# Q and k by 256-column matmuls in two PSUM banks, and the first column pairs of both retention output projections by seven products

## The chip, the cores and the metric

One core of one Trainium2 chip runs the kernel. The metric is the device time of one execution in microseconds (us). Three runs of the kernel before took 1381.68, 1379.70 and 1380.17 us; their median is 1380.17 us. The profile comes from one further execution.

## What is computed

A trunk of two layers over 256 tokens (`SEQ`) of width 2048 (`D`), all in float32: a gated linear attention layer (GLA, 4 heads) and a retention layer (8 heads). Each normalises its input, projects it to q, k, v and a gate, mixes the tokens head by head, multiplies by the gate's SiLU and projects back, with a residual add:

```python
def retention_mixer(h, positions, w_in, gn_g, gn_b, w_out):
    proj = h @ w_in
    q, k, v, gate = jnp.split(proj, [RET_DK, 2 * RET_DK, 2 * RET_DK + D_INNER], axis=-1)
    ...
    return (o * jax.nn.silu(gate)) @ w_out

def reference(x, ...):
    h = x
    for i in range(DEPTH):
        ...
            h = h + gla_mixer(rms_norm(h, gla_norm[j]), ...)
        ...
            h = h + retention_mixer(rms_norm(h, ret_norm[j]), ...)
    return rms_norm(h, final_norm)
```

With 256 tokens nearly all the work is in the projections: the input projections (2048 x 10240 for GLA, 2048 x 12288 for retention) and the two output projections (4096 x 2048).

## The kernel before

**Splitting.** Every float32 factor is split into a high part and a low part (`hi`, `lo`), and each product is the sum of three matmuls, high by high, high by low and low by high. `xhl` holds both parts of the layer's input for all 16 blocks of 128 rows (`kt`), `ogt` those of the gated output of the current half of the heads. Weights come as blocks of 256 rows by 512 columns (512 KB). SP loads a block into one of eight buffers (`emit_raw`, L228), ScalarE copies it to `hi` (L283), VectorE subtracts to get `lo` (L284). The order of all blocks is planned ahead by `_plan` (L56): `loads` is the order of the loads, `subs` the order of use. Splits run three blocks ahead of the matmuls (`LOOK`), loads at least six (`DMA_LOOK`).

**Plain column groups.** `steps_x` (L330) takes a block, and for each of two token halves `t` and two row blocks `q` issues three matmuls of 512 columns (`mm3`, L321 to L323): 12 matmuls of 512 columns per block, 8 blocks per group of 512 output columns.

**Pairs by seven products.** Two column groups that need the same input (v and gate of one head, or two neighbouring output columns) can be computed together on their first 1024 rows by Strassen's scheme: the upper four row blocks of both, for both token halves, make a two by two product of blocks, done in seven products instead of eight. `product` (L397) takes two combined weight blocks and issues 12 matmuls; `direct` (L404) takes the four remaining blocks of each group plainly. Tokens in order `P1 v4 z P3 ...` say which comes when: P1 to P8 are the products, v4 to v7 and g4 to g7 the plain blocks of the two groups. Weights are combined by DMAs on GpSimd's queue that add a second block into a loaded one (L292, `post`) and by VectorE adds (L278); the input is combined by `make_sums` (L420), which builds four token sums with their splits, called f3, f5, f6, f7. A pair takes 84 + 96 = 180 matmuls where two plain groups take 192, and 22 splits where they take 16. `JOINT` (L152) says which column groups go in pairs: `("ro", half)` is the retention output projection of a half of the heads, with one entry for columns 0 and 1 and one for columns 2 and 3.

**Q and k.** `step_w` (L342) computes q and k of a head transposed: the weights stand in the array, and the 256 tokens stream through. For each of four output blocks `c` and two row blocks it issues one matmul with the high weights over 512 columns (high and low part of x side by side, L364) and one with the low weights over 256 columns (L365). Each `c` has a PSUM bank of its own, with two halves of 256 columns; `evac_w` (L377) and `qk_done` (L1250) add the two halves: a ScalarE copy (L1257) and a VectorE add (L1258) for each `c`. There are 12 heads, 8 blocks each: 768 such pairs of matmuls.

**Order around the change.** GLA heads 0 and 1 (`gla_head`), the first half of the GLA output projection (`out_half`, tiles `gae`), GLA heads 2 and 3, its second half, then retention heads 0 to 3, the output projection `ra` of that half, heads 4 to 7, `rb`, and `out_tail`. Within a retention head the order is `WHOLE` for heads 0 and 4 (all q and k first) and `MIXED` for the others. The rest of a head (`ret_tasks`: scores, norm, transposes into `ogt`) is cut into steps that `step` runs between matmul blocks of the head itself and of what comes next. In `ra` and `rb`, columns 0 and 1 run plainly, first six blocks of each and then the last two (`CUT`), so that the last head's output has time to arrive; the residual is read back (`get_resid`) between these. In `ra`, columns 2 and 3 are a pair, its token sums (`rsum`) being made in steps during head 3 and `ra`'s first columns; `rb` has no pair. PSUM has eight banks: four named by `slots` (`acc`), two in the pool `lev`, two in `mis`.

## Time and profile before

| | |
|---|---|
| median of three runs | 1380.17 us |
| the profiled execution: its own time | 1379.47 us |
| its span, first to last instruction | 1377.6 us |
| busy: TensorE matmuls | 1366.5 us in 6632 records |
| busy: VectorE, ScalarE | 1079.1 us, 836.0 us |
| granted TensorE clock, mean | 0.998 |

In the profile PE is TensorE's matmuls, PEld its weight loads (they overlap the matmuls), DVE is VectorE, ACT ScalarE, POOL GpSimd, SP the engine that issues most loads. A line of the timeline gives start and duration in us. A matmul's duration holds its passage through the array, which overlaps the next matmul's: how fast matmuls follow each other is read from their starts, not from their durations. In a table by windows, the number behind x counts what touches the window, and the last three columns are the granted clock, the share of the 16 DMA engines that was busy, and what they moved.

### The profile page before, as it was taken

How to read it: one execution, taken by the hardware profiler on the slowest of the kernel's cores; microseconds unless marked ns; L12 is line 12 of the kernel's file. 1: busy time of each engine (PE TensorE's matmuls, PEld its weight loads, DVE VectorE, ACT ScalarE, POOL GpSimd, SP SyncE). 2: the span in 40 equal slices, each digit the busy share in tenths (PEclk: the TensorE clock that was granted, in tenths of full speed). 3: DMA queues.
4: the chain of work that ended last, by engine and by line, in shares of the span. 5: the costliest groups of instructions: out<-in, count | busy, mean ns of one | idle time of the engine just before them, and what ended most of it. 6: DMA issues, size and time to landing. Idle time of an engine off the chain costs nothing.

```text
span 1377.6 us, 18438 instructions
## 1 busy us (share of the span) xinstructions
PE 1366.5 (99%) x6632; PEld 1148.5 (83%) x6632; DVE 1079.1 (78%) x1497; ACT 836.0 (61%) x1104; POOL 131.8 (10%) x188
## 2 busy tenths in 40 slices
PE   9999999999999999999999999999999999999997
PEld 7888888888888888888888888888888888888887
DVE  6686795987878896769888888886858897888673
ACT  6576656656567747656666566655546666666452
POOL 1003020110021021001011010100101101010000
PEclk9999999999999999999999999999999999999999
DMA  9765556689658657858897878896798797879661
GB/s 359 245 182 160 172 177 187 151 250 343 204 153 265 204 175 180 314 168 247 279 317 202 256 203 247 208 310 206 184 372 238 217 271 193 256 199 327 211 191 62
DMA packets 83931, 312.94 MB, mean 227 GB/s; under 512 B 9712, under 2 KB 10736, under 8 KB 82560
## 3 DMA queue, kind: packets, MB, share of 16 engines
q1 hardware_dynamic: 67344, 242.64, 50.9%
q0 software_dynamic: 15056, 61.74, 22.6%
q10 hardware_dynamic: 1440, 7.38, 1.4%
q8 instruction: 52, 0.85, 0.2%
q14 instruction: 39, 0.32, 0.1%
HBM read 301.24 MB, written 10.49 MB: 226 GB/s over the span
## 4 chain that ended last, share of the span: by engine, by line
PE 99%; DMA 0%; DVE 0%; ACT 0%; DVEq 0%; issue 0%; SPq 0%
PE rqk_ps L364 8%; PE re_ps L392 8%; PE re_ps L391 8%; PE re_ps L393 8%; PE rqk_ps L365 4%; PE gqk_ps L364 4%; PE gg_ps L322 3%; PE gv_ps L321 3%; PE gv_ps L322 3%; PE gv_ps L323 3%; PE gg_ps L323 3%; PE gg_ps L321 3%; PE ge_ps L392 2%; PE ge_ps L393 2%; PE ge_ps L391 2%; PE gae_ps L391 2%
## 5 line engine op out<-in xcount | busy, mean ns | idle before, releaser
L284 DVE TENSOR_TENSOR lo<-raw,hi 128x1024 fp32r<-128x1024 f32 (+1 forms) x557 | 675.2, 1222 | 225.7 <-ACT hi L283 218.9
L283 ACT ACTIVATE hi<-raw 128x1024 fp32r<-128x1024 f32 (+1 forms) x557 | 584.5, 1056 | 390.8 <-PE gg_ps L323 49.0
L364 PE MATMUL rqk_ps<-xhl,hi 128*128 128x512 f32 x480 | 162.8, 397 | 0.0
L392 PE MATMUL re_ps<-lo,xhl 128*128 128x512 f32 x352 | 137.3, 390 | 0.0
L393 PE MATMUL re_ps<-hi,xhl 128*128 128x512 f32 x352 | 137.1, 390 | 0.0
L391 PE MATMUL re_ps<-hi,xhl 128*128 128x512 f32 x352 | 132.7, 391 | 0.0
L292 POOL DMA_DIRECT2D raw<-in_w_all x84 | 72.7, 867 | 530.3 <-DVE lo L284 283.8
L365 PE MATMUL rqk_ps<-xhl,lo 128*128 128x256 f32 x480 | 122.3, 280 | 0.0
L364 PEld LDWEIGHTS rqk_ps<-xhl,hi 128*128 128x128 f32 x480 | 89.5, 188 | 17.9
L365 PEld LDWEIGHTS rqk_ps<-xhl,lo 128*128 128x128 f32 x480 | 87.5, 189 | 3.4
L393 PEld LDWEIGHTS re_ps<-hi,xhl 128*128 128x128 f32 x352 | 66.1, 188 | 13.6
L391 PEld LDWEIGHTS re_ps<-hi,xhl 128*128 128x128 f32 x352 | 66.1, 188 | 13.3
L392 PEld LDWEIGHTS re_ps<-lo,xhl 128*128 128x128 f32 x352 | 66.1, 188 | 13.1
L364 PE MATMUL gqk_ps<-xhl,hi 128*128 128x512 f32 x216 | 76.5, 398 | 0.0
L322 PE MATMUL gg_ps<-lo,xhl 128*128 128x512 f32 x192 | 75.4, 393 | 0.0
L322 PE MATMUL gv_ps<-lo,xhl 128*128 128x512 f32 x192 | 75.2, 392 | 0.0
L321 PE MATMUL gv_ps<-hi,xhl 128*128 128x512 f32 x192 | 75.1, 393 | 0.0
L323 PE MATMUL gv_ps<-hi,xhl 128*128 128x512 f32 x192 | 75.0, 391 | 0.0
L323 PE MATMUL gg_ps<-hi,xhl 128*128 128x512 f32 x192 | 74.9, 390 | 0.0
L321 PE MATMUL gg_ps<-hi,xhl 128*128 128x512 f32 x192 | 74.8, 391 | 0.0
L365 PE MATMUL gqk_ps<-xhl,lo 128*128 128x256 f32 x216 | 59.0, 280 | 0.0
L801 POOL TENSOR_TENSOR s<-s,m 128x64 f32<-128x64 f32 x56 | 36.1, 676 | 232.7 <-DVE m L792 223.4
(407 smaller groups left out, 2682.5 us busy)
## 6 DMA issues: line engine op xcount, KB each, us to landing
raw<-in_w_all SPq DMA_DIRECT2D x451, 512.0 KB, 4.8
raw<-in_w_all POOLq DMA_DIRECT2D x84, 512.0 KB, 6.5
resid<-in_x_n SPq DMA_DIRECT2D x2, 1024.0 KB, 9.1
gg<-in_gn_g POOLq DMA_DIRECT2D x8, 256.0 KB, 3.9
resid_x<-resid ACTq DMA_DIRECT2D x1, 2048.0 KB, 9.1
gb<-in_gn_b POOLq DMA_DIRECT2D x8, 256.0 KB, 6.2
gb_resid<-resid_x POOLq DMA_DIRECT2D x1, 2048.0 KB, 11.8
resid_g<-gb_resid ACTq DMA_DIRECT2D x1, 2048.0 KB, 8.9
```

The lines of the kernel that those rows point to most:

```text
L283: a = nc.scalar.activation(hi[:, sl], src[:, sl], AF.Copy)
L284: b = nc.vector.tensor_tensor(lo[:, sl], src[:, sl], hi[:, sl].bitcast(F32), ALU.subtract)
L292: nc.gpsimd.dma_start(raws[n], block(key), accum_op=ALU.add)
L321: mm(ps, xh, hi[:, q, :], start=kt == 0, stop=False)
L322: mm(ps, xh, lo[:, q, :], start=False, stop=False)
L323: mm(ps, xl, hi[:, q, :], start=False, stop=kt == NKT - 1)
L364: mm(ps[c], wh, rhs[:, kt, :, :], start=kt == 0, stop=False)
L365: mm(ps[c][:, 0, :], wl, rhs[:, kt, 0, :], start=False, stop=False)
L391: mm(ps, xh, hi[:, q, :], start=start, stop=False, **again)
L392: mm(ps, xh, lo[:, q, :], start=False, stop=False, **again)
L393: mm(ps, xl, hi[:, q, :], start=False, stop=stop, **again)
L801: nc.gpsimd.tensor_tensor(dst, dst, side_of(m[:, li, :], z), ALU.add)
```

## The change

Three things are changed.

1. **Q and k.** Each pair of matmuls (512 and 256 columns) becomes three of 256: high weights by the high part of x, high weights by the low part, low weights by the high part, all three into the same 256 columns of PSUM. Two blocks `c` share a bank, so that q and k of a head take two banks instead of four. The two halves need not be added afterwards: two ScalarE copies of 512 columns replace four copies and four VectorE adds.
2. **Pairs.** `("ro", 0)` becomes (True, True) and `("ro", 1)` (True, False): columns 0 and 1 of `ra` and of `rb` are pairs (tiles `rae`, `rbe`). They run in the order `LATE`, in which the plain blocks of the last head (v6, v7, g6, g7) come late and the second gate accumulator has a bank of its own in `lev`. `CUT` is gone.
3. **Token sums.** They are made in head 2 of each half (heads 2 and 6) instead of around `ra`; two of the four go to DRAM at once (`spill_sums`) and come back at the end of heads 3 and 7 (`back_sums`). `get_resid` moves to v7 of those heads. In the order `MIXED`, P2 comes before q4, and P5 gets bank C.

How the order of instructions changes at three places (names with numbers are single tiles; `hi` and `lo` are the split weight blocks).

TensorE, in the q and k of retention head 0 (`rqk_ps` are its accumulators, one for each output block before, one for two blocks after): before, a high matmul of 512 columns and a low one of 256 alternate,

```order
L364 MATMUL rqk_ps_5767<-xhl,hi_5801 128x512
L365 MATMUL rqk_ps_5767<-xhl,lo_5802 128x256
L364 MATMUL rqk_ps_5764<-xhl,hi_5801 128x512
L365 MATMUL rqk_ps_5764<-xhl,lo_5802 128x256
L364 MATMUL rqk_ps_5765<-xhl,hi_5801 128x512
L365 MATMUL rqk_ps_5765<-xhl,lo_5802 128x256
```

and now:

```order
L365 MATMUL rqk_ps_5984<-xhl,hi_5942 128x256
L366 MATMUL rqk_ps_5984<-xhl,hi_5942 128x256
L368 MATMUL rqk_ps_5984<-xhl,lo_5943 128x256
L365 MATMUL rqk_ps_5984<-xhl,hi_5942 128x256
L366 MATMUL rqk_ps_5984<-xhl,hi_5942 128x256
L368 MATMUL rqk_ps_5984<-xhl,lo_5943 128x256
```

The columns are the same, 768 for each block; there are three instructions for them instead of two, and the first two carry the same weights.

TensorE, where the first half of the GLA output projection begins (`gg_ps` is the last gate of head 1, `got_tp` are transposes of a head's output, `gae_ps` the first product P1; the brackets name what an instruction waits for): before,

```order
L323 MATMUL gg_ps_2118<-hi_2230,xhl 128x512
L679 MATMUL got_tp_2267<-ident,go_1984 128x128 [waits DVE_49]
L679 MATMUL got_tp_2295<-ident,go_1984 128x128
L391 MATMUL gae_ps_2326<-hi_2250,ogt 128x512 [waits Activation_49]
L679 MATMUL got_tp_2267<-ident,go_1984 128x128 [waits DVE_49]
L679 MATMUL got_tp_2267<-ident,go_1984 128x128 x2
L679 MATMUL got_tp_2295<-ident,go_1984 128x128 x3
```

and now:

```order
L333 MATMUL gg_ps_2228<-hi_2340,xhl 128x512
L709 MATMUL got_tp_2377<-ident,go_2094 128x128 [waits DVE_49]
L709 MATMUL got_tp_2405<-ident,go_2094 128x128
L709 MATMUL got_tp_2377<-ident,go_2094 128x128 [waits DVE_49]
L709 MATMUL got_tp_2377<-ident,go_2094 128x128 x2
L709 MATMUL got_tp_2405<-ident,go_2094 128x128 x3
L400 MATMUL gae_ps_2436<-hi_2360,ogt 128x512 [waits Activation_49]
```

Since GLA head 0 now takes two banks of `slots` where it took four, the groups after it lie in the other two banks: P1's bank is now that of the gate just finished, and P1 stands behind all eight transposes.

GpSimd's queue of DMAs, from the end of head 3 through `ra` (`raw` rows are weight blocks that are added into loaded ones; `resid` is the residual, `dm`, `gg`, `gb` are constants of the next head): before,

```order
L460 DMA ra_resid<-resid_g 128x4096
L1162 DMA dm_9376<-in_dmat 128x384
L1169 DMA gb_9403<-in_gn_b 128x512
L1168 DMA gg_9823<-in_gn_g 128x512
L292 DMA raw_8374<-in_w_all 128x1024
L292 DMA raw_8394<-in_w_all 128x1024
```

and now:

```order
L490 DMA resid_8540<-resid_g 128x4096
L1206 DMA dm_9900<-in_dmat 128x384
L447 DMA rsum_8682<-rsum_kept 128x2048
L1213 DMA gb_9927<-in_gn_b 128x512
L300 DMA raw_8495<-in_w_all 128x1024
L300 DMA raw_8507<-in_w_all 128x1024
L1212 DMA gg_10401<-in_gn_g 128x512
L300 DMA raw_8581<-in_w_all 128x1024
L300 DMA raw_8593<-in_w_all 128x1024
L300 DMA raw_8495<-in_w_all 128x1024
L300 DMA raw_8507<-in_w_all 128x1024
```

The six adding DMAs of the first pair (`raw_8495` to `raw_8593`) and the return of the two spilled sums (`rsum_8682`) are new; those of the second pair (`raw_8374` before) follow behind them.

The diff, cut to its core:

```diff
--- before.py
+++ after.py
@@ _plan
-                        post.append((x[j], (g, 2 + j)))
+                        (owed if " ".join(order) == LATE else post).append((x[j], (g, 2 + j)))
...
-    def out_cols_of(name, half, cut, joint):
+    def out_cols_of(name, half, joint):
...
-MIXED = "q0 q1 P1 q2 q3 q4 z P5 q5 P6 q6 q7 P2 P3 v4 v5 v6 P7 v7 g4 g5 P8 g6 g7"
+MIXED = "q0 q1 P1 q2 q3 P2 q4 z P5 q5 P6 q6 q7 P3 v4 v5 v6 P7 v7 g4 g5 P8 g6 g7"
...
+LATE = "v4 g4 P1 v5 z P3 g5 P5 v6 P6 P2 g6 P7 v7 g7 P8"
...
-CUT = 6
 EARLY = 2
 JOINT = {
     "a": (5, 7),
     ("ao", 0): (True, True),
     ("ao", 1): (False, True),
-    ("ro", 0): (False, True),
-    ("ro", 1): (False, False),
+    ("ro", 0): (True, True),
+    ("ro", 1): (True, False),
 }
@@ step_w
+        at = lambda c: ps[c // 2][:, c % 2, :]
+        both = lambda c: {"skip_group_check": c % 2 == 1}
...
-            if kt == NKT - 1:
-                mm(ps[c][:, 0, :], wl, rhs[:, kt, 0, :], start=False, stop=False)
-                mm(ps[c], wh, rhs[:, kt, :, :], start=False, stop=True)
-            else:
-                mm(ps[c], wh, rhs[:, kt, :, :], start=kt == 0, stop=False)
-                mm(ps[c][:, 0, :], wl, rhs[:, kt, 0, :], start=False, stop=False)
+            a = [
+                lambda c=c, wh=wh, kt=kt: mm(at(c), wh, rhs[:, kt, 0, :], start=kt == 0 and c % 2 == 0, stop=False, **both(c)),
+                lambda c=c, wh=wh, kt=kt: mm(at(c), wh, rhs[:, kt, 1, :], start=False, stop=False, **both(c)),
+            ]
+            b = [lambda c=c, wl=wl, kt=kt: mm(at(c), wl, rhs[:, kt, 0, :], start=False, stop=kt == NKT - 1, **both(c))]
...
-        ps = ps or acc(4, f"{name}_ps", (P, 2, SEQ))
+        ps = acc(2, f"{name}_ps", (P, 2, SEQ))
...
-    def evac_w(ps, dst, name):
-        tmp = t4_p.tile([P, 4, SEQ], F32, tag="t4", name=f"{name}_h2")
+    def evac_w(ps, dst):
         with tc.high_priority():
-            for c in range(4):
-                nc.scalar.activation(tmp[:, c, :], ps[c][:, 1, :], AF.Copy)
-                halves = lambda a: a.rearrange("p (z t) -> p z t", z=2)
-                to = dst[:, c // 2, :].rearrange("p (z k t) -> p z k t", z=2, k=2)[:, :, c % 2, :]
-                nc.vector.tensor_tensor(to, halves(ps[c][:, 0, :]), halves(tmp[:, c, :]), ALU.add)
+            for i in range(2):
+                to = dst[:, i, :].rearrange("p (z k t) -> p k z t", z=2, k=2)
+                nc.scalar.activation(to, ps[i].rearrange("p k (z t) -> p k z t", z=2), AF.Copy)
@@ make_sums
+    def sums_apart(name):
+        def room(n):
+            if n == 0:
+                return v_p.tile([P, 2, QK, 2, P], F32R, tag="v", name=f"{name}0")
+            return [t4_p.tile([P, QK, 2, P], F32R, tag="t4", name=f"{name}_t{i}") for i in range(2)]
+
+        return room
+
+    def spill_sums(name):
+        kept = dram_p.tile([P, 2 * QK * 2 * P], F32R, tag=name, name=f"{name}_kept")
+        for i in range(2):
+            nc.gpsimd.dma_start(
+                kept[:, i * QK * 2 * P : (i + 1) * QK * 2 * P], cur["next_s"][2 + i].rearrange("p k a t -> p (k a t)")
+            )
+        cur["spilt"] = kept
+
+    def back_sums(name):
+        two_ = v_p.tile([P, 2, QK, 2, P], F32R, tag="v", name=f"{name}1")
+        nc.gpsimd.dma_start(two_.rearrange("p i k a t -> p (i k a t)"), cur["spilt"])
+        cur["next_s"][2:4] = [two_[:, 0], two_[:, 1]]
+
+    def make_sums(lhs, name, where, key="s"):
+        s = cur[key] = [None] * 4
         room = where(name)
@@ out_pair
+        order = out_order(name[0] + "o", c)
+        G1 = A
+        if order == LATE:
+            G1 = lev_p.tile([P, GW], F32, tag="lev", name=f"{name}e{c}_g1")
...
+        toks = [x for x in order.split() if x != "z"]
+        for n, tok in enumerate(toks):
+            if tok[0] == "P":
+                products[tok]()
+            else:
...
+            if n < 4:
+                advance()
+                step()
+                if n == 3:
+                    drain_side()
...
@@ ret_head
-        at = (2, 3, 0, 1) if h < 4 else (0, 1, 2, 3)
-        q_ps = [acc(1, f"rqk{h}_ps{c}", (P, 2, SEQ), [at[c + 2]])[0] for c in range(2)]
-        q_ps += [lev_p.tile([P, 2, SEQ], F32, tag="lev", name=f"rqk{h}_ps{c}") for c in (2, 3)]
-        if not mixed:
-            q_ps = q_ps[2:] + q_ps[:2]
+        at = (2, 3, 0, 1)
+        q_ps = [lev_p.tile([P, 2, SEQ], F32, tag="lev", name=f"rqk{h}_ps{c}") for c in range(2)]
...
-            tmp = t4_p.tile([P, 4, SEQ], F32, tag="t4", name=f"rqk{h}_h2")
-            for c in range(4):
-                nc.scalar.activation(tmp[:, c, :], q_ps[c][:, 1, :], AF.Copy)
-                nc.vector.tensor_tensor(qk[:, c, :], q_ps[c][:, 0, :], tmp[:, c, :], ALU.add)
+            for i in range(2):
+                nc.scalar.activation(qk[:, 2 * i : 2 * i + 2, :], q_ps[i], AF.Copy)
...
-        drain = toks.index("P2" if mixed else "v5")
+        drain = toks.index("q7" if mixed else "v5")
+
+        last = h % 4 == 3
+        making = make_sums(ogt, f"rsum{h}", sums_apart, "next_s") if h % 4 == 2 else None
 
         def turn(tok):
             n = toks.index(tok)
+            if making and tok in ("q3", "P2", "q4", "P5", "q5"):
+                next(making)
+                if tok == "q5":
+                    spill_sums(f"rsum{h}")
+            if last and tok == "v7":
+                get_resid(f"resid{h}")
...
+                if last and tok == "g7":
+                    back_sums(f"rsum{h}")
...
@@ tile_trunk_kernel
-    tasks.append(make_sums(ogt, "rsum", sums_in_v))
-    out_half(True, False, "ra", CUT, out_steps, JOINT["ro", 0])
+    cur["s"] = cur["next_s"]
+    out_half(True, False, "ra", JOINT["ro", 0])
...
-    out_half(False, True, "rb", CUT, out_steps)
+    slots = deque((0, 1, 2, 3))
+    cur["s"] = cur["next_s"]
+    out_half(False, True, "rb", JOINT["ro", 1])
```

212 lines of the change are left out of this document (107 added, 105 removed).

## The prediction

> **What bounds the kernel now.** I read the page's busy times first, then the chain that ended last, then the timeline of TensorE where the change works. The page:
>
> ```profile
> span 1377.6 us, 18438 instructions
> ...
> PE 1366.5 (99%) x6632; PEld 1148.5 (83%) x6632; DVE 1079.1 (78%) x1497; ACT 836.0 (61%) x1104; POOL 131.8 (10%) x188
> ...
> PE 99%; DMA 0%; DVE 0%; ACT 0%; DVEq 0%; issue 0%; SPq 0%
> ```
>
> The third line is the chain: followed back from its end, the kernel is TensorE's stream and nothing else. So an edit counts by what it adds to that stream or takes from it, and work moved off VectorE or ScalarE counts only where it made TensorE wait. Since durations overlap, the price of a matmul is the distance of starts. Here is the stream in the q and k of a retention head:
>
> ```profile
> 800.32 0.40 PE L364 MATMUL rqk_ps<-xhl,hi 128*128 128x512 f32 x1
> 800.55 0.28 PE L365 MATMUL rqk_ps<-xhl,lo 128*128 128x256 f32 x1
> 800.67 0.40 PE L364 MATMUL rqk_ps<-xhl,hi 128*128 128x512 f32 x1
> ...
> 801.27 0.28 PE L365 MATMUL rqk_ps<-xhl,lo 128*128 128x256 f32 x1
> 801.38 0.40 PE L364 MATMUL rqk_ps<-xhl,hi 128*128 128x512 f32 x1
> ```
>
> A 512 is followed after 0.23, a 256 after 0.11 to 0.12, and from 800.32 to 801.38 three pairs pass: 0.353 us each. Now three windows: two hold nothing but q and k, the third nothing but the matmuls of 256 columns in the kernel's tail.
>
> ```profile
> 134.70:146.00 11.30, 11.30 (x66) 9.77 (x64) 8.71 (x21) 5.67 (x9) 0.00 (x0) 1.00 0.58 186
> 1011.40:1033.70 22.30, 22.30 (x128) 19.39 (x127) 11.03 (x12) 9.52 (x11) 2.28 (x3) 1.00 0.99 344
> 1346.50:1369.30 22.80, 22.80 (x192) 22.80 (x190) 6.57 (x21) 5.24 (x13) 0.00 (x0) 1.00 0.13 47
> ```
>
> By the weight loads, which have fewer edges: 64 in 11.30 us and 127 in 22.30 us give 0.353 and 0.351 us for a pair, so 0.352; 190 in 22.80 us give 0.120 us for a 256 among 256s.
>
> Last, plain matmuls of 512 columns, the first and the last of 28 in a row:
>
> ```profile
> 1334.71 0.39 PE L323 MATMUL rb_ps<-hi,ogt 128*128 128x512 f32 x1
> ...
> 1340.83 0.39 PE L323 MATMUL rb_ps<-hi,ogt 128*128 128x512 f32 x1
> ```
>
> 27 distances in 6.12 us: 0.227 us each. Twice 0.120 less 0.227 leaves 0.013 us: that much of a matmul does not grow with its columns, so a cut in two costs it once more.
>
> **The change, part by part.**
>
> *Q and k.* Each of 768 pairs becomes three 256s. The tail is the same thing in another place: three matmuls in a row into the same 256 columns of PSUM, two of them with the same weights. Three take 0.360 us, 0.008 us more than the pair; times 768 that is +6.1 us. The first 256 behind a 512 followed after 0.11 instead of 0.12 (801.27 above); this happens about once in each of 96 blocks and takes back 0.7 us. I take **+5.5 us**. The ends are the two pair rows: against 0.353 it is 768 x 0.007 less 0.7, +4.7 us; against 0.351, without the edge, +6.9 us.
>
> *Pairs.* Two pairs of 180 matmuls stand where 2 x 192 stood: 24 fewer at 0.227 us, **-5.4 us**. The two big terms cancel.
>
> *The changed banks at the GLA projection.* Before, this is what happens there:
>
> ```profile
> 250.35 1.39 ACT L659 ACTIVATE gsg<-gg_ps,rr 128x512 f32<-128x512 f32 x2 [0.98 <-PE gg_ps L323]
> ...
> 250.84 0.38 PE L679 MATMUL got_tp<-ident,go 128*128 128x128 f32 x2
> 250.97 0.48 PE L391 MATMUL gae_ps<-hi,ogt 128*128 128x512 f32 x1
> 251.29 0.82 PE L679 MATMUL got_tp<-ident,go 128*128 128x128 f32 x6
> ...
> 251.87 0.48 PE L392 MATMUL gae_ps<-lo,ogt 128*128 128x512 f32 x1
> ```
>
> The two SiLUs read the last gate's banks until 251.74. P1's first matmul did not wait for them; now its bank is the second one's. Eight transposes stand ahead of it, which fill 250.84 to about 251.8, so they hide the wait, and the one matmul that used to start early is lost: **+0.2 us**. Without that cover it would be half the SiLU row, 0.7 us; nothing speaks for a gain. Behind P1 on TensorE all else queues, so this counts in full.
>
> *The lighter evacuation of q and k.* It drops these from all retention heads, and the same from the GLA heads:
>
> ```profile
> L1257 ACT ACTIVATE rqk_h<-rqk_ps x32: 365/385/391, 677.4 to 1244.4; 128x256 f32<-128x256 f32 x32
> L1258 DVE TENSOR_TENSOR rqk<-rqk_ps,rqk_h x32: 414/418/426, 678.7 to 1244.9; 128x256 f32<-128x256 f32 x32
> ```
>
> That is 12 x 4 x 0.418 = 20 us of VectorE. TensorE never waited for it (99% of the chain), so it is worth 0. The 12 more splits of the pairs and one more set of sums take as much back.
>
> *Token sums.* They move into heads 2 and 6. One set is, by these rows, 2 x 1.22 + 4 x 0.69 + 4 x 0.68 = 7.9 us of VectorE:
>
> ```profile
> L427 DVE TENSOR_TENSOR rsum_y<-ogt x2: 1220/1220/1220, 905.1 to 909.4; 128x1024 f32<-128x1024 f32 x2
> L433 DVE TENSOR_TENSOR rsum_f<-rsum_f,rsum_y x1: 690/690/690, 915.8 to 915.8; 128x512 f32<-128x512 f32 x1
> L443 DVE TENSOR_TENSOR rsum<-rsum_f,rsum x4: 683/684/686, 951.0 to 954.4; 128x512 fp32r<-128x512 f32 x4
> ```
>
> I price this and the new DMAs at 0, behind the splits that run three blocks ahead; what they cost without that cover is worked out under the rivals. Neither can gain, since there is no wait of TensorE to remove.
>
> *Sum*, against the profiled execution (1379.47 us: the span and 1.9 us around it): 5.5 - 5.4 + 0.2 = +0.3 us, 1379.8 us. The profiled execution lay 0.7 us below the median; on the median it is **1380.5 us**. By the ends of the terms, +4.7 - 5.4 + 0 to +6.9 - 5.4 + 0.7, it is 1379.5 to 1382.4 us.
>
> **The rivals.** No change means within 0.2%, 1377.4 to 1382.9 us, about what a measurement of this kernel can tell from none.
>
> *Weight blocks come late in the first pairs (slower).* The place is head 3 and the first pair of `ra`, and the same in `rb`. Head 2, head 3, `ra`'s plain columns and its pair, before:
>
> ```profile
> 838.00:880.00 42.00, 42.00 (x213) 35.57 (x212) 38.02 (x55) 27.91 (x39) 4.31 (x6) 1.00 0.75 219
> 880.00:921.60 41.60, 41.60 (x200) 34.93 (x199) 36.45 (x44) 25.57 (x32) 3.70 (x5) 1.00 0.94 286
> 921.60:970.20 48.60, 48.60 (x220) 40.29 (x219) 34.34 (x51) 24.79 (x33) 2.86 (x4) 1.00 0.74 214
> 970.20:1011.40 41.20, 41.20 (x184) 34.12 (x183) 34.59 (x34) 23.97 (x23) 3.45 (x4) 1.00 0.85 263
> ```
>
> In the second and third, the DMA engines are busy 0.94 x 41.6 + 0.74 x 48.6 = 75.1 us of 90.2. What comes in addition goes through GpSimd's queue, q0 (packets, MB, share of the time of 16 engines):
>
> ```profile
> q1 hardware_dynamic: 67344, 242.64, 50.9%
> q0 software_dynamic: 15056, 61.74, 22.6%
> ```
>
> 0.226 x 1377.6 us over 61.74 MB is 2.64 us for 512 KB. Six adding DMAs and 1 MB of returning sums are 8 x 2.64 = 21 us: 96 us of work in a stretch that shrinks to 87.5 us, 8.7 us too much. It decides from the point where this overrun exceeds the cover: three blocks ahead are, in products of six matmuls a block, 3 x 6 x 0.227 = 4.1 us. Then TensorE waits 4.6 us: **1385.1 us**. For it speaks also a row of the waits:
>
> ```profile
> ACT hi L283 <- DMA raw<-in_w_all: 47.4, 28, 4.4
> ```
>
> Splits already wait for blocks, up to 4.4 us. Against it: TensorE idled for none of these 28, up to eight buffers fill ahead while plain blocks of 2.7 us pass, and the queue's mean price is high for transfers with free time behind them in the next window (0.15 x 41.2 = 6 us). Chance 0.15.
>
> *VectorE is full in heads 2 and 6 (slower).* In the first of the four windows it is busy 38.02 us of 42.00. With 7.9 us of sums, and 1.7 us (4 x 0.418) less evacuation, that is 44.2 us: 2.2 us too much, twice, **1384.9 us** if all of it reaches TensorE. Against it: the splits' cover of over 4 us, and heads 3 and 7, which get lighter. Chance 0.07.
>
> *The third matmul is free (faster).* If a triple took the pair's 0.352 us, only the pairs and the bank would count: -5.2 us, **1375.0 us**. For it: both kinds stream the same 768 columns. Against it: the tail row. The Trainium skill's page "TensorE: Matmul & The Clock Gate", section "Back-to-back issue gap", leans this way: a warm gap is the columns at 2.4 GHz and 2.5 ns, so that cutting a 512 in two costs 2.5 ns; by it the sum would be 768 x 0.0025 - 24 x 0.2158 + 0.2 = -3.1 us, 1377.1 us as an estimate. The trace disagrees with it: 0.227 and 0.120 us where it has 0.216 and 0.109. Chance 0.06.
>
> *The second high matmul needs no weight load (faster).* It has the same weights as the first. If the 0.013 us went with the load, 768 x 0.013 = 10 us would go: **1370.5 us**. Against it, the tail's loads, where L321 and L322 share theirs:
>
> ```profile
> L323 PEld LDWEIGHTS tail_ps<-xhl,ogt 128*128 128x128 f32 x64 | 12.3, 192 | 0.0
> L322 PEld LDWEIGHTS tail_ps<-tail,ogt 128*128 128x128 f32 x63 | 12.1, 192 | 0.0
> L321 PEld LDWEIGHTS tail_ps<-xhl,ogt 128*128 128x128 f32 x63 | 12.1, 192 | 0.0
> ```
>
> Every matmul has its own load. Chance 0.04.
>
> **How the numbers follow.** The forecast, no change at 1380.5 us, has 0.68. Slower: 0.15 + 0.07 = 0.22. Faster: 0.06 + 0.04 = 0.10. The range goes up past the two slow rivals, to 1385.5 us, and down to 1377.0 us, a little beyond the point where the third matmul is half free (1377.7 us); it leaves out most of the fast cases and some of the slow ones.
>
> **What would show it.** A window of pure q and k in the new trace with 0.120 us a matmul shows the first term, 0.117 us (a third of 0.352) refutes it. The three matmuls' weight loads should be equal in number. The first pairs of `ra` and `rb` should hold 180 matmuls 0.227 us apart, and a start of `gae` near 251.8 us after allowance for the shift. Idle time or long distances in the pairs, with splits waiting for weight blocks, would mean the DMA rival; the same in heads 2 and 6, with splits behind sums on VectorE, the other. The forecast is wrong if these exceed 2.4 us together, or if a 256 in q and k costs less than 0.1187 us (3.1 us less over 2304 matmuls).

## The result and the profile after

The changed kernel takes **1382.89 us** (median of 20 runs, 1381.73 to 1384.89), the kernel before 1380.16 us (20 runs beside it, 1378.41 to 1384.03): a ratio of 1.0020, with a 95% interval of 1.0013 to 1.0027. So it is about 2.7 us slower, clear of the scatter and just at the border of what was called no change; it lies inside the range on record and 2.4 us above the forecast.

The profiled execution of the changed kernel took 1383.86 us, 1.0 us above its median; that of before lay 0.7 us below its own. The two traces therefore differ by 4.4 us where the medians differ by 2.7. The page of the changed kernel, the lines that answer to those of before, and the row of the adding DMAs:

```profile
span 1382.1 us, 19965 instructions
...
PE 1369.5 (99%) x7376; PEld 1186.0 (86%) x7376; DVE 1089.2 (79%) x1481; ACT 847.8 (61%) x1098; POOL 145.9 (11%) x206
...
q1 hardware_dynamic: 66768, 240.55, 49.1%
q0 software_dynamic: 17648, 72.23, 25.0%
...
PE 94%; DMA 3%; DVE 1%; issue 1%; ACT 1%; POOL 0%; DVEq 0%; SPq 0%; ACTq 0%; POOLq 0%
...
raw<-in_w_all POOLq DMA_DIRECT2D x96, 512.0 KB, 7.5
```

TensorE is still busy for 99% of the span, with 744 more matmuls. What is new is in the chain: DMA, VectorE and ScalarE have 5% of it, where before it hardly left TensorE. Somewhere TensorE now waits for a transfer and a split; everything else has to be found in the distances of matmul starts.

**Q and k.** A window of the changed kernel, in the second half of the GLA layer, that holds nothing but q and k (busy time and count of PE, weight loads, VectorE, ScalarE, GpSimd, then clock and DMA):

```profile
337.00:359.00 22.00, 22.00 (x185) 22.00 (x185) 12.73 (x15) 9.59 (x10) 0.00 (x0) 1.00 0.84 317
```

And TensorE's timeline in the q and k of another head, where transposes (L709) stand among them:

```profile
143.65 0.28 PE L368 MATMUL gqk_ps<-xhl,lo 128*128 128x256 f32 x1
143.77 0.38 PE L709 MATMUL got_tp<-ident,go 128*128 128x128 f32 x2
143.91 0.36 PE L365 MATMUL gqk_ps<-xhl,hi 128*128 128x256 f32 x1
144.11 0.28 PE L366 MATMUL gqk_ps<-xhl,hi 128*128 128x256 f32 x1
144.22 0.28 PE L368 MATMUL gqk_ps<-xhl,lo 128*128 128x256 f32 x1
```

185 weight loads touch 22.00 us, some 0.12 us each, as in the tail. But the matmul behind the two transposes is followed after 0.20 us (143.91 to 144.11) instead of 0.12. Such a long distance stands behind every stretch of transposes. With all q and k starts of the trace past the first 15 us (the first 11 are at half clock): 2256 matmuls in 271.59 us, so **0.3612 us for three**; before, 752 pairs in 264.62 us, **0.3519 us** each. Without the long ones, 18 after and 15 before, each of them behind a 128-column matmul, it is 0.3591 and 0.3503 us. Over the whole kernel q and k went from 272.70 to 279.75 us, +7.05 us.

The groups of weight loads (duration least, median and most, first and last start) show that each of the three matmuls has its own, in equal numbers:

```profile
L365 PEld LDWEIGHTS rqk_ps<-xhl,hi x512: 186/192/192, 653.8 to 1253.5; 128*128 128x128 f32 x171
L366 PEld LDWEIGHTS rqk_ps<-xhl,hi x512: 187/192/192, 653.9 to 1253.6; 128*128 128x128 f32 x171
L368 PEld LDWEIGHTS rqk_ps<-xhl,lo x512: 187/192/192, 659.2 to 1253.8; 128*128 128x128 f32 x171
```

**Pairs.** By their starts, all of `rb` takes 62.75 us where it took 65.52: -2.77 us, as it should. All of `ra` takes 83.53 where it took 84.53: -1.00 us, so 1.8 us are missing there. TensorE's timeline in the second pair of `ra`:

```profile
997.06 0.39 PE L401 MATMUL rae_ps<-lo,ogt 128*128 128x512 f32 x1
997.29 0.39 PE L402 MATMUL rae_ps<-hi,ogt 128*128 128x512 f32 x1
998.49 0.50 PE L400 MATMUL rae_ps<-hi,ogt 128*128 128x512 f32 x1 [0.81 <-ACT hi L291]
999.40 0.50 PE L400 MATMUL rae_ps<-hi,rsum 128*128 128x512 f32 x1 [0.41 <-DVE resid L1016]
```

ScalarE's splits there:

```profile
993.46 1.06 ACT L291 ACTIVATE hi<-raw 128x1024 fp32r<-128x1024 f32 x1 [1.48 <-DMA raw<-in_w_all]
996.43 2.00 ACT L291 ACTIVATE hi<-raw 128x1024 fp32r<-128x1024 f32 x2 [1.91 <-DMA raw<-in_w_all]
```

From 997.29 to 999.40 pass two matmuls instead of nine. ScalarE could not start the splits at 993.46 and 996.43 earlier, because adding DMAs landed only then: the third and the fourth of this pair's six were issued at 985.84 and 988.10 us and landed 7.5 and 8.2 us later. The second of TensorE's two waits is for a VectorE add (L1016), which stood behind the late block's split. It is the only wait of this size in the trace that before does not have.

**The banks at the GLA projection.** TensorE's timeline at the transposes and the start of P1:

```profile
251.88 1.03 PE L709 MATMUL got_tp<-ident,go 128*128 128x128 f32 x8
252.82 0.50 PE L400 MATMUL gae_ps<-hi,ogt 128*128 128x512 f32 x1
253.16 0.39 PE L401 MATMUL gae_ps<-lo,ogt 128*128 128x512 f32 x1
253.38 0.40 PE L402 MATMUL gae_ps<-hi,ogt 128*128 128x512 f32 x1
```

P1 starts at 252.82, 0.94 us behind the first transpose, and its first matmul is followed after 0.34 us. From the first transpose to P1's third matmul, which has the same work ahead of it in both kernels, pass 1.50 us (251.88 to 253.38); before it was 1.34 (250.84 to 252.18). So the new banks cost 0.16 us.

### The profile page after: what moved, and what is told of

The parts are those of the page before. It is cut to its first block, busy times and chain, and to the rows that moved or that the text cites. A ratio compares the mean times of both kernels' runs of the same rounds, so it can differ in the third digit from the quotient of the medians.

```text
span 1382.1 us, 19965 instructions
## 1 busy us (share of the span) xinstructions
PE 1369.5 (99%) x7376; PEld 1186.0 (86%) x7376; DVE 1089.2 (79%) x1481; ACT 847.8 (61%) x1098; POOL 145.9 (11%) x206
## 4 chain that ended last, share of the span: by engine, by line
PE 94%; DMA 3%; DVE 1%; issue 1%; ACT 1%; POOL 0%; DVEq 0%; SPq 0%; ACTq 0%; POOLq 0%
PE re_ps L401 8%; PE re_ps L400 8%; PE re_ps L402 8%; PE rqk_ps L368 4%; PE rqk_ps L366 4%; PE rqk_ps L365 4%; DMA raw<-in_w_all 3%; PE gg_ps L332 3%; PE gv_ps L333 3%; PE gv_ps L329 3%; PE gv_ps L332 3%; PE gg_ps L329 3%; PE gg_ps L333 3%; PE gqk_ps L365 2%; PE gqk_ps L368 2%; PE gqk_ps L366 2%
## 5 line engine op out<-in xcount | busy, mean ns | idle before, releaser
L292 DVE TENSOR_TENSOR lo<-raw,hi 128x1024 fp32r<-128x1024 f32 (+1 forms) x569 | 688.7, 1221 | 222.1 <-ACT hi L291 216.6
L291 ACT ACTIVATE hi<-raw 128x1024 fp32r<-128x1024 f32 (+1 forms) x569 | 597.7, 1056 | 398.3 <-PE rqk_ps L366 61.0
L366 PE MATMUL rqk_ps<-xhl,hi 128*128 128x256 f32 x512 | 144.0, 283 | 0.0
L365 PE MATMUL rqk_ps<-xhl,hi 128*128 128x256 f32 x512 | 143.9, 283 | 0.0
L300 POOL DMA_DIRECT2D raw<-in_w_all x96 | 83.2, 867 | 547.1 <-DVE lo L292 302.7
L368 PE MATMUL rqk_ps<-xhl,lo 128*128 128x256 f32 x512 | 140.3, 283 | 0.0
L365 PEld LDWEIGHTS rqk_ps<-xhl,hi 128*128 128x128 f32 x512 | 97.9, 191 | 1.9
L366 PEld LDWEIGHTS rqk_ps<-xhl,hi 128*128 128x128 f32 x512 | 98.0, 191 | 1.4
L368 PEld LDWEIGHTS rqk_ps<-xhl,lo 128*128 128x128 f32 x512 | 96.0, 192 | 0.7
L402 PEld LDWEIGHTS re_ps<-hi,xhl 128*128 128x128 f32 x352 | 66.1, 188 | 13.3
L365 PE MATMUL gqk_ps<-xhl,hi 128*128 128x256 f32 x256 | 73.2, 289 | 1.3 <-ACT hi L291 1.3
```

Source lines behind the costliest of these rows:

```text
L291: a = nc.scalar.activation(hi[:, sl], src[:, sl], AF.Copy)
L292: b = nc.vector.tensor_tensor(lo[:, sl], src[:, sl], hi[:, sl].bitcast(F32), ALU.subtract)
L300: nc.gpsimd.dma_start(raws[n], block(key), accum_op=ALU.add)
L365: lambda c=c, wh=wh, kt=kt: mm(at(c), wh, rhs[:, kt, 0, :], start=kt == 0 and c % 2 == 0, stop=False, **both(c)),
L366: lambda c=c, wh=wh, kt=kt: mm(at(c), wh, rhs[:, kt, 1, :], start=False, stop=False, **both(c)),
L368: b = [lambda c=c, wl=wl, kt=kt: mm(at(c), wl, rhs[:, kt, 0, :], start=False, stop=kt == NKT - 1, **both(c))]
```

## The experiments

The theory after reading the two traces: each triple costs 0.0092 us more than the pair, wherever it stands (+7 us); the pairs give 5.4 us; a late adding DMA takes about 1.7 of them back; the rest is worth nothing. The main rival: the parts act on each other, so that the 7 us belong to the new surroundings, or VectorE or the DMA engines set the price of the sums.

Each kernel was timed beside the kernel before on the same chip (1380.62 us in the first four runs, 1380.86 in the next four, 1381.25 in the next three, 1381.11 in the last).

### Q and k alone

The kernel before with the new `step_w`, `evac_w` and `qk_done`, and the banks turned back:

```diff
...
+        if h == 0:
+            slots.rotate(2)
```

> The kernel before with only q and k changed: three 256-column matmuls in two banks and the light evacuation; no new pairs, old token sums, and the banks turned by two behind GLA head 0, so that the groups after it lie where they lay before. Theory (the triple costs more than the pair, all through): the accounting of the two traces gives q and k 7.05 us more, 0.0092 us for each of 768 triples. So 1380.2 + 7.0 = 1387.2 us, 1386.2 to 1388.2, with 0.361 us a triple in the trace and no new wait elsewhere. Rival 1 (the 7 us belong to the changed surroundings, such as other DMAs and sums beside q and k, and by themselves the triples cost what the tail row forecast): 1385.7 us, with 0.1197 us a matmul and few long distances. Rival 2 (the light evacuation gives time back that no wait of the trace showed): under 1385 us.

Measured: **1387.48 us** (1384.82 to 1387.98), ratio 1.0042 (1.0029 to 1.0056), so +6.9 us. In its trace a triple takes 0.3614 us (2254 matmuls), and 19 distances behind transposes are long. By the trace the theory holds and both rivals fall: the triples cost this much in the old surroundings too, 0.0095 us more than the pairs, and the lighter evacuation gave nothing back. The medians alone would not decide: their interval is +4.0 to +7.7 us, and rival 1 stood at +5.5. One thing was not expected: in the one pair that `ra` had already before, TensorE waited 0.9 us, at the same product where the changed kernel waits, though no DMA of this kernel was changed, and 1.1 us more in `gae` (at 329 us). So the +6.9 us are not the price of the triples alone.

### The pairs alone

The changed kernel with the old q and k; in the heads:

```diff
...
-            for i in range(2):
-                nc.scalar.activation(qk[:, 2 * i : 2 * i + 2, :], q_ps[i], AF.Copy)
+            tmp = t4_p.tile([P, 4, SEQ], F32, tag="t4", name=f"rqk{h}_h2")
+            for c in range(4):
+                nc.scalar.activation(tmp[:, c, :], q_ps[c][:, 1, :], AF.Copy)
+                nc.vector.tensor_tensor(qk[:, c, :], q_ps[c][:, 0, :], tmp[:, c, :], ALU.add)
```

> The changed kernel with the q and k of before (512 and 256 columns, four banks, ScalarE copy and VectorE add); the first pairs, the early token sums and the moved residual stay, and the order of mixed heads is that of before. Theory (pairs give 5.4 us, one stall in the second pair of ra takes 1.8 back): 1380.2 - 5.4 + 1.8 = 1376.6 us, 1375.8 to 1377.4. Rival 1 (without q and k the stall goes, since it came from the lighter head 3 reaching ra sooner relative to its loads): 1374.8 us. Rival 2 (with the old evacuation back, VectorE is full in heads 2 and 6 where the sums are made, up to 2.2 us each): 1378 to 1381 us, with idle time of TensorE in those heads.

Measured: **1393.92 us** (1391.79 to 1396.09), ratio 1.0092 (1.0076 to 1.0107): 13.3 us slower than before, where the theory had 4 us faster. None of the three was right in size; rival 2 was right about the place. TensorE stands still in head 2 at 826 us and in head 6 at 1188 us. Three windows, ahead of the first of these waits, in it, and behind it (columns as above, the granted clock third from the end):

```profile
820.00:826.20 6.20, 6.20 (x34) 5.24 (x32) 6.20 (x8) 3.79 (x4) 0.79 (x1) 1.00 0.83 300
826.20:832.60 6.40, 0.38 (x2) 0.02 (x1) 6.40 (x10) 4.18 (x10) 1.66 (x4) 0.81 0.90 167
832.60:836.90 4.30, 4.29 (x10) 3.43 (x11) 1.12 (x4) 1.23 (x2) 0.38 (x1) 0.50 1.03 331
```

TensorE's timeline there:

```profile
826.19 0.39 PE L403 MATMUL re_ps<-hi,xhl 128*128 128x512 f32 x1
832.61 0.77 PE L401 MATMUL re_ps<-hi,sums 128*128 128x512 f32 x1 [6.03 <-DVE rqk L1307]
833.17 0.63 PE L402 MATMUL re_ps<-lo,sums 128*128 128x512 f32 x1
833.60 0.63 PE L403 MATMUL re_ps<-hi,sums 128*128 128x512 f32 x1
```

The next product waits for the evacuation of q and k (L1307), because its bank is one of theirs. Behind the wait the clock is granted at half, and ten matmuls stand about 0.43 us apart, which costs two more microseconds. VectorE is busy all the time, but what is late is ScalarE's copy of q and k, by its timeline:

```profile
831.56 1.21 ACT L1306 ACTIVATE rqk_h<-rqk_ps 128x256 f32<-128x256 f32 x4 [2.22 <-DVE rsum L474]
```

The q and k were complete at about 824 us. The copy goes into `rqk_h`, a tile of the pool `t4`; that pool has four buffers, the token sums use them too, and the copy starts when one of the last VectorE operations on the sums (L474) lets one go. Whether the buffer is the reason is tried next.

### The same, without the buffer

```diff
-            tmp = t4_p.tile([P, 4, SEQ], F32, tag="t4", name=f"rqk{h}_h2")
             for c in range(4):
-                nc.scalar.activation(tmp[:, c, :], q_ps[c][:, 1, :], AF.Copy)
-                nc.vector.tensor_tensor(qk[:, c, :], q_ps[c][:, 0, :], tmp[:, c, :], ALU.add)
+                nc.scalar.activation(qk[:, c, :], q_ps[c][:, 1, :], AF.Copy)
+                nc.vector.tensor_tensor(qk[:, c, :], q_ps[c][:, 0, :], qk[:, c, :], ALU.add)
```

> The kernel of e2_pairs_alone with one edit: the evacuation of q and k in the retention heads copies the second half of a bank straight into its place in q and k, and VectorE adds the first half in place; it takes no buffer of the pool t4 any more. In e2_pairs_alone TensorE stood 6.4 us at 826 and at 1188 us, then ran 10 matmuls 0.427 us apart. Theory (a buffer, not VectorE's time: the four t4 buffers are held by the token sums, so the evacuation's copy waits for a sum to be finished, and the banks of q and k stay full): both stalls go, with the slow matmuls behind them, and pairs give their 5.4 us less the stall of 1.7 in the second pair of ra: 1380.6 - 5.4 + 1.7 = 1376.9 us, 1375.5 to 1378. Rival (VectorE has no room in heads 2 and 6 for sums and adds together, 2.2 us too much in each, which the forecast had as a rival): at least 2 us of idle TensorE stay in each of the two heads, and the time is above 1380 us.

Measured: **1377.60 us** (1376.20 to 1379.72), ratio 0.9975 (0.9965 to 0.9985). ScalarE's timeline in the same head, the first and the last of the four copies:

```profile
820.21 0.37 ACT L1305 ACTIVATE rqk<-rqk_ps 128x256 f32<-128x256 f32 x1
...
822.17 0.38 ACT L1305 ACTIVATE rqk<-rqk_ps 128x256 f32<-128x256 f32 x1 [0.31 <-PE rqk_ps L372]
```

They now wait for TensorE alone, and run ahead of the sums. Both long waits are gone, with the slow matmuls behind them; only 0.6 us stay in head 2 (at 839 us). VectorE does the same operations as in e2_pairs_alone, so it was the buffer that cost 16 us, not VectorE's time. And the version is 3.3 us faster than before and over 5 us faster than the changed kernel: the pairs' gain does not need the 256-column q and k. (0.9 us of waits in `gae` and 1.3 in the second pair of `ra` are still in its trace.)

### 256 columns in two heads only

e2_pairs_alone with the new q and k where the sums are made:

```diff
...
+        light = h % 4 == 2
-        q_ps = [acc(1, f"rqk{h}_ps{c}", (P, 2, SEQ), [at[c + 2]])[0] for c in range(2)]
+        q_ps = [] if light else [acc(1, f"rqk{h}_ps{c}", (P, 2, SEQ), [at[c + 2]])[0] for c in range(2)]
...
```

> The kernel of e2_pairs_alone, but with the 256-column q and k in two banks and the light evacuation in retention heads 2 and 6, where the token sums are made; all other heads keep the pairs of 512 and 256. Theory: 128 triples cost 128 x 0.0092 = 1.2 us, the stalls of heads 2 and 6 go, the second pair of ra keeps its 1.7 us: 1380.6 - 5.4 + 1.2 + 1.7 = 1378.1 us, 1377 to 1379.3; that is 12 us better than e2_pairs_alone and about 5.5 us better than the changed kernel, since ten heads don't pay. Rival (the stalls come from the sums themselves): as in e2_pairs_alone, over 1390 us.

Measured: **1378.13 us** (1376.36 to 1379.32), ratio 0.9979 (0.9970 to 0.9988), to 0.1 us what was expected; with an interval of 1.2 us to either side, that it came so near is luck. It says the same from the other side: the light evacuation is worth much in heads 2 and 6 once the sums are there, and nothing in the ten other heads, where the triples only cost. A window of this kernel around the sums has VectorE (third pair of columns) busy without a gap, and TensorE too:

```profile
820.00:836.90 16.90, 16.90 (x93) 14.70 (x93) 16.90 (x21) 11.27 (x15) 2.83 (x4) 1.00 0.93 262
```

### The wait in the second pair of `ra`: order of the adding DMAs

```diff
-                        (owed if " ".join(order) == LATE else post).append((x[j], (g, 2 + j)))
+                        (owed if g[0] == "ro" else post).append((x[j], (g, 2 + j)))
```

> The changed kernel with one edit in the plan: also in the second pair of ra, the adding DMAs for P7's block are posted behind those of the block that P3, P5 and P6 use, as the first pairs have it already. Theory (a chain of latencies: the adding DMAs for P6's and P5's blocks sit behind the others in GpSimd's queue and land 3 to 4 us too late): the stall of 1.8 us near 998 us shrinks below 0.5, and the time is 1382.9 - 1.5 = 1381.4 us. Rival (the DMA engines lack room there, whatever the order): the stall stays between 1.3 and 2.3 us and the time is 1382.9 us within 0.5.

Measured: **1383.18 us** (1382.12 to 1384.19), ratio 1.0015 (1.0007 to 1.0024). This run tests neither theory. The edit changes the plan, but not one instruction: the adding DMAs of that pair stood in this order on GpSimd's queue already, and the program is the changed kernel's. Its trace has the same four issues at the same distances, 2.27, 0.90 and 1.30 us. What it gives is the scatter: the wait is 1.0 us here and 1.7 in the changed kernel's own trace, and one program has the medians 1383.18 and 1382.89 us.

### The banks turned back

```diff
+        if h == 0:
+            slots.rotate(2)
```

> The changed kernel with the four banks turned by two behind GLA head 0, so that P1 of the first GLA output projection has a bank that the last gate doesn't use, as before. Theory (the bank costs what the accounting gives at gae, 0.26 to 0.34 us at its first half): P1's first matmul stands ahead of the last six transposes again, and the time is 0.3 us less, 1382.6 us, a difference only the trace can show. Rival (the order of transposes does not matter): gae starts as late as in the changed kernel, 1382.9 us.

Measured: **1384.23 us** (1381.73 to 1387.43), ratio 1.0026 (1.0016 to 1.0036). TensorE's timeline at the place:

```profile
251.34 0.38 PE L709 MATMUL got_tp<-ident,go 128*128 128x128 f32 x2
251.48 0.48 PE L400 MATMUL gae_ps<-hi,ogt 128*128 128x512 f32 x1
251.79 0.82 PE L709 MATMUL got_tp<-ident,go 128*128 128x128 f32 x6
252.37 0.48 PE L401 MATMUL gae_ps<-lo,ogt 128*128 128x512 f32 x1
252.68 0.39 PE L402 MATMUL gae_ps<-hi,ogt 128*128 128x512 f32 x1
```

P1's first matmul is ahead of six transposes again, as before, and from the first transpose to the third matmul it is 1.34 us again, so the extra 0.16 us are gone from the trace. The median, expected 0.3 us lower, is 1.3 us higher; the intervals of the two ratios overlap, and this trace has a wait of 0.8 us in head 2 (at 842) that the changed kernel's lacks. The mechanism of the term is shown, its worth only by the trace.

### The second pair in the order `LATE`

```diff
-    return LATE if (name, c) == ("ro", 0) else UNIT
+    return LATE if name == "ro" else UNIT
```

> The changed kernel with the second pair of ra in the order LATE too, nothing else. Theory (the stall at 997 us is lead time that the adding DMAs lack, and it is 1.0 to 1.7 us of the 2.7 by which the changed kernel is slower): the stall goes and the time is 1382.9 - 1.5 = 1381.4 us. Rival (the stall has no part in the medians): 1382.9 us within 0.5.

> e5_in_place, and the second pair of ra in the order LATE too, which puts the plain blocks g4 and g5 ahead of P1 and P5 and so gives the adding DMAs of P5 and P6 some 5 us more. Theory: the stall of 0.9 to 1.7 us in the second pair goes, so 1380.6 - 5.4 = 1375.2 us, 1374.3 to 1376.5, the best version. Rival (the DMA engines are behind there whatever comes first): the stall moves to another product and the time is that of e5_in_place within 0.5 us.

Measured: e8_late_second **1383.39 us** (1381.46 to 1384.60), ratio 1.0016 (1.0007 to 1.0025); e7_in_place_late **1376.80 us** (1375.82 to 1377.75), ratio 0.9970 (0.9958 to 0.9982). In both traces the wait in `ra` is gone, and all of `ra` has its full gain (81.70 and 81.72 us, -2.8). The time does not follow: e8_late_second has smaller waits at 1066, 1197 and 1317 us (0.7 us together), e7_in_place_late three in head 4. ScalarE's timeline of e7_in_place_late ahead of the first of those:

```profile
1039.19 1.06 ACT L291 ACTIVATE hi<-raw 128x1024 fp32r<-128x1024 f32 x1 [3.31 <-DMA raw<-in_w_all]
1042.43 2.01 ACT L291 ACTIVATE hi<-raw 128x1024 fp32r<-128x1024 f32 x2 [2.18 <-DMA raw<-in_w_all]
```

Taking away this wait gave nothing that the medians show: 1376.80 against 1377.60 us and 1383.39 against 1382.89 us lie within each other's intervals. The rival of e8_late_second had it right. The time of e7_in_place_late is 0.8 us under e5_in_place, below the rival's 0.5 and above the theory's range; that the waits came up elsewhere is what the rival said.

### Less for the DMA engines in `ra`

e7_in_place_late, with `post` and `owed` empty for the second pair of `ra`, so that this version leaves out what the six DMAs add:

```diff
+        bare = g == ("ro", 0, 3)
...
-                        (owed if " ".join(order) == LATE else post).append((x[j], (g, 2 + j)))
+                        ([] if bare else owed if " ".join(order) == LATE else post).append((x[j], (g, 2 + j)))
-                    use(z[j] if tok in ("P3", "P7") else x[j], z[j] if tok == "P6" else None, post)
+                    use(z[j] if tok in ("P3", "P7") else x[j], z[j] if tok == "P6" else None, [] if bare else post)
```

> e7_in_place_late without the six adding DMAs of the second pair of ra: the weight blocks of its products P3, P5, P6 and P7 lack what the DMAs would add, all else is computed and timed as before. Theory (the DMA engines are behind in ra, and what isn't waited for in ra is waited for in head 4: e7_in_place_late waited 2.1 us there, at 1043 to 1062): with 6 x 2.64 = 15.8 us less of their time, the waits of ra and head 4 are both gone, and the time is 1376.8 - 2.1 = 1374.7 us. Rival (head 4 waits for something else, such as its own adding DMAs behind the constants in GpSimd's queue): the waits at 1043 to 1062 stay, 1376.8 us within 0.5.

Measured: **1376.34 us** (1375.36 to 1377.21), ratio 0.9968 (0.9956 to 0.9980), 0.5 us under e7_in_place_late. Two of the three waits of head 4 stayed, 0.7 us each. Late there are that head's own adding DMAs, beside the 2 MB of its returning sums, by the DMA issues from 1018 to 1046 us (KB each, median us to landing):

```profile
sums<-sums_kept POOLq DMA_DIRECT2D x1, 2048.0 KB, 12.8
raw<-in_w_all POOLq DMA_DIRECT2D x2, 512.0 KB, 12.7
```

The rival is nearer: two of head 4's three waits do not come from the adding DMAs of `ra`. The third, 0.6 us, went with them; by one trace that may be scatter.

### The order of sizes in q and k

e5_in_place with four 512s, then four 256s:

```diff
...
+                for c in range(4):
+                    keep(mm(ps[c], hi[:, q, c * P : (c + 1) * P], rhs[:, kt, :, :], start=kt == 0, stop=False))
+                for c in range(4):
+                    keep(mm(ps[c][:, 0, :], lo[:, q, c * P : (c + 1) * P], rhs[:, kt, 0, :], start=False, stop=False))
```

> e5_in_place with the q and k of the middle blocks in another order: four high matmuls of 512 columns, then four low ones of 256, where 512 and 256 alternated (some 560 of the 768 pairs). It asks what the price of a 256 and of a 512 is beside which neighbour, since the first term of the forecast rested on that. In the trace of before a 512 takes 0.234 us ahead of a 256 and 0.227 to 0.231 ahead of a 512, a 256 0.117 to 0.120. Theory (a change of size costs some ns): a group of four pairs takes 1.390 to 1.395 us instead of 1.403, so 1.1 to 1.8 us go: 1377.6 - 1.4 = 1376.2 us. Rival (768 columns and two instructions have one price in any order): a pair stays 0.3515 us on average and the time 1377.6 us.

> e7_in_place_late with the order of e9_grouped: what the parts give together. Theory: 1376.8 - 1.4 = 1375.4 us, better than every other version; rival (the sizes' order gives nothing, or what it gives is waited for at the next block): 1376.8 us within 0.5.

Measured: e9_grouped **1411.12 us** (1405.38 to 1411.63), ratio 1.0210 (1.0192 to 1.0229); e11_grouped_late **1409.28 us** (1408.30 to 1410.20), ratio 1.0206 (1.0192 to 1.0220). Theories and rivals all missed by 32 us or more. `keep` pins a matmul to its place in the program, so that the scheduler could no longer let matmuls pass side work that wasn't ready. TensorE's timeline in e9_grouped, behind q and k of a GLA head:

```profile
134.55 0.63 PE L372 MATMUL gqk_ps<-xhl,lo 128*128 128x256 f32 x4
139.45 0.66 PE L718 MATMUL got_tp<-ident,go 128*128 128x128 f32 x2 [4.26 <-issue]
140.73 1.54 PE L718 MATMUL got_tp<-ident,go 128*128 128x128 f32 x6 [0.62 <-DVE go L906]
143.84 1.08 PE L718 MATMUL got_tp<-ident,go 128*128 128x128 f32 x4 [1.57 <-DVE ogt L519]
```

The same grouping without `keep`:

> e9_grouped without the pin on the program order of the grouped matmuls, so that transposes and other side work may again be moved between them. In e9_grouped the trace has 0.232 us ahead of a 512 or a 256 for each 512 of q and k, and 0.118 us for each 256, whatever follows: 0.350 us a pair, as the alternating order has it. Theory (the order of sizes is worth next to nothing, and the 33 us of e9_grouped are waits at the pinned order: 4.5 us at the transposes of 134.9, 2 us at each of eight places, and the slow matmuls behind them): 1377.6 - 0.4 = 1377.2 us, 1376 to 1378.4. Rival (grouping itself makes the waits, since all of a block's high and low weights are needed sooner): above 1390 us.

Measured: **1375.37 us** (1374.59 to 1376.71), ratio 0.9961 (0.9948 to 0.9975). So the 33 us came with the pin. The time is 0.6 us below the theory's range. The price of q and k is what the theory said: 0.3517 us a pair in the grouped order (752 pairs), 0.3519 in the alternating one. Nor does the rest of the trace say why the median should beat that of e5_in_place by 2.2 us: the two profiled executions took 1376.36 and 1376.25 us. The intervals of the two ratios overlap, and the difference is not taken for shown. As the fastest version run it is 5.7 us under before.

## Why the prediction was right or wrong

**The bound** was right: TensorE's stream decides, and each term that counted was read from matmul starts.

**Q and k, +5.5 us forecast, +7.05 us by the trace.** The mechanism was right, the size just above the upper end of its bounds (+6.9). The step that was mis-sized is "three take 0.360 us, 0.008 us more than the pair", by the price of the pair. The triple's 0.360 us, less the 0.7 us taken off it, is what q and k showed without long distances (0.3591 us). The pair's 0.352 us came from two windows that are dearer than the average: by matmul starts a pair takes 0.353 us in both, with no transpose ahead of any. In another head's q and k of the kernel before, ten pairs pass in 3.47 us, 0.347 each:

```profile
337.40 0.39 PE L364 MATMUL gqk_ps<-xhl,hi 128*128 128x512 f32 x1
...
340.87 0.39 PE L364 MATMUL gqk_ps<-xhl,hi 128*128 128x512 f32 x1
```

Over the whole kernel a pair takes 0.3503 us without the long distances. So the difference was 0.0088 us and not 0.0071, 1.3 us over 768, and three more matmuls behind transposes make the other 0.25 us. That 0.352 is also the mean of all pairs with the long distances in it (0.3519) is a coincidence. Why a pair takes 0.347 us in one stretch and 0.353 in another is not shown by any run.

**Pairs, -5.4 us.** Right: -2.77 us in `rb`, and -2.8 in `ra` where no wait stands in it (e7_in_place_late, e8_late_second). In the changed kernel 1.7 us of the gain go to the wait in the second pair.

**The banks, +0.2 us.** Right: 0.16 us, and gone with the banks turned back.

**"Worth 0" for the evacuation and "0" for the sums.** Each zero held by itself (e1_qk_alone gained nothing by the first; the changed kernel pays nothing for the second), but the step that failed in the working is that the parts were priced one by one. The sums cost nothing here because the light evacuation leaves `t4` to them: with the old evacuation the two together cost 16 us (e2_pairs_alone against e5_in_place). The result did not suffer, since the change makes both; the prediction did not say that one needs the other.

**The DMA rival (1385.1 us).** Its mechanism came, at another place and smaller: not the first pairs of `ra` and `rb` but the second pair of `ra`, 1.7 us instead of 4.6. The overrun was worked out for a whole head and a projection against a cover of three blocks; what is late in fact are two adding DMAs of one pair, issued when the blocks that they add to are there and landing 7.5 and 8.2 us later. Issue and landing both have a part. The second of the two is issued 2.3 us behind the first, since it waits for a VectorE add (L286), where the kernel before has 1.1 us; and in e1_qk_alone, with the 1.1 us of before, it landed after 10.4 us where before it took 8.4. Whether the delay is the chain of these latencies or the DMA engines' rate in those 15 us stays open: e3_owed is the same program, and e8_late_second and e10_no_adding only show that waits at other places follow. Nor does the median follow this wait, so how much of the 2.7 us is due to it is not settled. Of the medians' 2.7 us, 7.05 - 5.45 + 0.16 = 1.8 are accounted for by the three terms; for the other 0.9 this wait and scatter are candidates, neither shown.

**VectorE full (1384.9 us).** Refuted: the changed kernel's trace has no wait of TensorE in heads 2 and 6, and e6_two_heads has VectorE busy for 16.9 us of 16.9 without one. That the splits' lead was the cover is likely, but no run varied it.

**The two fast rivals.** Refuted by 0.3591 us a triple where a free third matmul would leave 0.352, and by equal numbers of weight loads. The estimate of 1377.1 us by 0.0025 us a cut falls with it: the cut cost 0.0088.

So the time lay inside the range, 2.4 us above the forecast, and it lay that near because the two large terms cancel. Of the 2.4 us 1.5 are in the first term, and the rest is not settled.

## What to carry to other kernels

Price a change's parts together where they share a pool: here a scratch buffer tied the cheap part (an evacuation off the critical path) to the dear one, and writing the copy in place gave the whole gain without the price. A term of some 700 small differences needs its prices from all of them: two windows read 0.352 us a pair where the whole kernel has 0.350, which was a fifth of the term here. An edit that is meant to change an order has to be found in the order of the instructions first: one here changed the plan and nothing else. And a wait that is taken away at one place is worth only what does not appear at the next: look at the median, not at the wait.

## What the runs showed of the hardware that was not expected

- **A matmul behind one of 128 columns**, mostly a transpose, takes about 0.08 us more until the next starts: all 15 long distances of q and k before, and all 18 after, stand there, and no matmul of q and k that stands there has a short one (0.20 instead of 0.12 us for 256 columns, 0.31 instead of 0.23 for 512).
- **At half clock the cut costs nothing.** TensorE's timeline of the changed kernel in the first 11 us:

```profile
6.42 0.41 PE L366 MATMUL gqk_ps<-xhl,hi 128*128 128x256 f32 x1
6.64 0.41 PE L365 MATMUL gqk_ps<-xhl,hi 128*128 128x256 f32 x1
```

And before:

```profile
8.35 1.91 PE L352 MATMUL gqk_ps<-xhl,hi 128*128 128x512 f32 x4
10.05 1.05 PE L354 MATMUL gqk_ps<-xhl,lo 128*128 128x256 f32 x4
10.90 0.63 PE L612 MATMUL zps<-xhl,wa 128*48 128x512 f32 x1
```

  A 256 takes 0.213 us there and a 512 0.425 (1.70 us for four), so four pairs and four triples both take 2.55 us. The 0.013 us a matmul that do not grow with its columns show only at full clock. By the Trainium skill's page "TensorE: Matmul & The Clock Gate", section "Part 1: The HAM clock gate", the starts of a cold array's matmuls lie as far apart as their columns take at 1.2 GHz, 0.427 us for 512; by that rule a 256 takes 0.213 us, an estimate. The trace agrees.
- **An idle TensorE costs twice.** 6.4 us of waiting in e2_pairs_alone were followed by ten matmuls at half clock (granted 0.50 for 4.3 us; as an estimate from the 0.81 in the window of the wait, the clock fell some 4 us into it), while the 1.2 us of the changed kernel at 997 us were not. The same section says that a window of about 3.4 us without work halves the clock, and that as long a busy one restores it: for this wait the trace agrees. But in e9_grouped much shorter waits were enough, by these two windows around its wait at 759.58 us:

```profile
759.60:762.90 3.30, 1.56 (x7) 1.05 (x7) 3.30 (x6) 1.54 (x2) 0.57 (x1) 1.00 0.95 359
762.95:766.35 3.40, 3.40 (x13) 2.70 (x12) 3.40 (x4) 1.65 (x2) 0.10 (x1) 0.50 0.92 223
```

  Two starts lie 2.19 us apart there, TensorE is busy for 1.56 us of 3.30, and the next 3.4 us have half the clock. This comes six times in that trace, each time behind a wait of 2.0 to 2.4 us between two starts. In e11_grouped_late three of seven such waits (at 760, 813 and 1032 us) were not followed by half clock; on what it depends no run shows.
